# Scan exponentials with a per-head bias, forward rows alone shifted ahead of the choice, in a two-layer Hyena, SSD and attention backbone on one core

## The chip, the core and the metric

The kernel runs on one core of a Trainium2 chip, as one program in one launch. The metric is device time in microseconds (us). Five engines run side by side, each through a queue of its own in the order in which the built program lists its instructions: TensorE (PE), VectorE (DVE), ScalarE (ACT), GpSimd (POOL), and SyncE (SP), which issues nearly all DMAs here. They wait for each other through semaphores.

## What is computed

Two layers over 512 latent tokens and 256 context tokens, width 1024. Each layer projects its normalised input into three groups of heads (a Hyena long convolution, a bidirectional Mamba-2 scan, a windowed attention), gates and concatenates them, projects back and normalises. The change lies in the scan. For one direction the reference computes, in chunks of 128 tokens:

```python
da = (dt * a).reshape(b, nc, SSM_CHUNK, h)
acs = jnp.cumsum(da, axis=2)
seg = acs[:, :, :, None, :] - acs[:, :, None, :, :]
decay_ls = jnp.exp(jnp.where(lower, seg, -jnp.inf))
y_diag = jnp.einsum("bclhn,bcshn,bclsh,bcshp->bclhp", Cc, Bc, decay_ls, xd)
...
y_f, s_f = _ssd_scan(xs, dt[:, :, 0], a[0], Bh, Ch, init_f)
y_b, s_b = _ssd_scan(flip(xs), flip(dt[:, :, 1]), a[1], flip(Bh), flip(Ch), init_b)
return y_f + flip(y_b), s_f, s_b
```

Within a chunk the forward direction fills the triangle of pairs on one side of the diagonal and the reversed direction the other one. So one 128x128 matrix per head can hold both: forward exponents in the one triangle, reversed exponents in the other. The step size dt is put into the exponent as its logarithm.

## The kernel before

Activations lie with channels on partitions and tokens along the free axis. Every fp32 product runs as three products of rounded parts (a high part, made by ACT, line 178; a low part, made by DVE, line 179), so TensorE does most of its work in the input projection (`proj`, lines 461 and 463: PSUM tiles `pl` for 512 latent tokens, `pc` for 256 context tokens), each block with its own weights (`wr`, loaded by line 439, split into `wh` and `wl`).

`ssm_in` projects the scan's inputs, applies a short convolution (`conv`, lines 530 to 543: ACT copies `pl` and `pc` out of PSUM in lines 532 and 536 and scales in 538, DVE does lines 539 and 540) and works out small per-token tables in the tile `sc`, eight tables of 128 x 96: 96 columns are 2 directions x 6 chunks x 8 heads, direction 0 (forward) in columns 0 to 47. Table 3 (`S2`, read as `LB`) is log(dt) minus the running sum of dt*a. The running sums as rows go to DRAM (`rd`).

`ssm` first scans the chunk states (lines 798 to 807), then takes the chunks one by one: 6 in layer 0, 4 in layer 1. A chunk makes `gm` (line 819, ACT) and `ys` (lines 829 to 838, DVE), transposes `ys` into the PSUM tile `py` (line 840), and then goes twice, for 4 heads each, through what is called a **pass** here:

1. SP loads `R` (128 partitions x 2 directions x 4 heads x 128, 512 KB) from `rd` (line 844). `R` has three buffers, so the load of a pass waits until the pass three before it has been read by line 854.
2. ACT adds `LB` to each head's rows, one instruction per direction and head (line 849, 8 in a pass).
3. DVE overwrites the reversed rows by the forward rows in the upper triangle (line 851).
4. ACT takes the exponential of all 4 heads at once (line 852, in place).
5. DVE multiplies with `gm` into `M` (line 854); then the buffer of `R` is free.
6. PE multiplies with x into `py` (line 858, 4 matmuls).

After both passes ACT copies `py` out (line 859) and SP stores it (line 860). There are 12 passes in layer 0 and 8 in layer 1. A scheduler sets the order of each engine's queue when the program is built: it places the instructions of all open work, so the scan's chunks stand between projections of the Hyena blocks (`hy_in`) and pieces of the next modulation (`modulation`, line 370; its 1 MB weight loads are line 365). A queue doesn't pass over an instruction that waits. Passes are told apart by the number of their buffer; in layer 0 before, passes 1 to 12 are R_833, 835, 846, 848, 861, 863, 876, 878, 891, 893, 906 and 908.

Of the kernel before, what the change touches and what calls it, by code (L numbers as in the profile page):

```python
# [12 lines left out]
AF = mybir.ActivationFunctionType  # L13
ALU = mybir.AluOpType
# [32 lines left out]
class Net:  # L47
# [642 lines left out]
    def ssm_in(self, l, xt, last):  # L690
        nc = self.nc
# [43 lines left out]
        X, Z, S, S2, DT, AC, TOT, DA = [sc[:, i] for i in range(8)]  # L735
# [39 lines left out]
        nc.vector.tensor_scalar_max(S2, DT, 1e-38)  # L775
        nc.scalar.activation(S2, S2, AF.Ln)
        nc.vector.tensor_tensor(S2, S2, AC, op=ALU.subtract)
        return xT, bt, bc, sc, rd

    def ssm(self, l, xT, bt, bc, sc, rd, last):  # L780

        nc = self.nc
        sp = self.dr.tile([4, P, QW], F32, name=self.nm("sp"))
        col = lambda c: c * P + (0 if c < 4 else 1)
        vec = lambda i, d, c: sc[:, i, (d * 6 + c) * 8:(d * 6 + c) * 8 + 8]
        W, EX, ET, LB, DT = 0, 1, 2, 3, 4
        h64 = lambda t: t.rearrange("p (h d) -> p h d", h=8)
        bc64 = lambda v: v.unsqueeze(2).to_broadcast([P, 8, 64])
        states = {}

        def scan(d, order):
            cur = None
            for i, c in enumerate(order):
                states[d, c] = cur
                if i == len(order) - 1:
                    break
                xw = self.w("xw", [P, 512], bufs=2)
                nc.vector.tensor_tensor(h64(xw), h64(xT[:, c]), bc64(vec(W, d, c)), op=ALU.mult)
                ps = self.wk()
                for g in range(2):  # L800
                    nc.tensor.matmul(ps[:, 256 * g:256 * g + 256], lhsT=bt[:, g, c], rhs=xw[:, 256 * g:256 * g + 256], start=True, stop=True)  # L801
                nxt = self.w(f"st{d}", [P, 512], bufs=5 if d else 3)
                if cur is None:
                    nc.vector.tensor_copy(nxt, ps)
                else:
                    nc.vector.tensor_tensor(h64(nxt), h64(cur), bc64(vec(ET, d, c)), op=ALU.mult)
                    nc.vector.tensor_tensor(nxt, nxt, ps, op=ALU.add)
                cur = nxt

        scan(1, [5, 4, 3, 2, 1, 0])  # L810
        scan(0, [4, 5, 0, 1, 2, 3])
        dcol = self.row[:, l, 40:48]
        for c in (0, 1, 2, 3) if last else (4, 5, 0, 1, 2, 3):
            q0 = col(c)
            pg = self.wk()
            for g in range(2):
                nc.tensor.matmul(pg[:, g * P:(g + 1) * P], lhsT=bc[:, g, q0:q0 + P], rhs=bc[:, 2 + g, q0:q0 + P], start=True, stop=True)
            gm = self.w("gm", [P, 2, P], bufs=2)
            nc.scalar.activation(gm, pg[:, 0:256].rearrange("p (g l) -> p g l", g=2), AF.Copy)

            own = self.ts([P, 10])
            for g in range(2):
                t = self.w("dg", [P, P])
                nc.vector.scalar_tensor_tensor(t, gm[:, g], 1.0, self.ident, op0=ALU.mult, op1=ALU.mult, accum_out=own[:, 8 + g:9 + g])
                w = slice(4 * g, 4 * g + 4)
                nc.vector.scalar_tensor_tensor(own[:, w], vec(DT, 1, c)[:, w], own[:, 8 + g:9 + g], dcol[:, w], op0=ALU.mult, op1=ALU.add)
            py = self.wk()
            ys = self.w("ys", [P, 512], bufs=3)
            nc.vector.tensor_tensor(h64(ys), h64(xT[:, c]), bc64(own[:, 0:8]), op=ALU.mult)
            for d in range(2):  # L830
                if states[d, c] is None:
                    continue
                po = self.wk()
                for g in range(2):
                    nc.tensor.matmul(po[:, 256 * g:256 * g + 256], lhsT=bc[:, 2 + g, q0:q0 + P], rhs=states[d, c][:, 256 * g:256 * g + 256], start=True, stop=True)
                yo = self.w("yo", [P, 512], bufs=3)
                nc.vector.tensor_tensor(h64(yo), h64(po), bc64(vec(EX, d, c)), op=ALU.mult)
                nc.vector.tensor_tensor(ys, ys, yo, op=ALU.add)
            for j in range(4):
                nc.tensor.matmul(py[:, j * P:(j + 1) * P], lhsT=ys[:, j * P:(j + 1) * P], rhs=self.ident, start=j == 0, stop=False, is_transpose=True, skip_group_check=True)  # L840

            for g in range(2):
                R = self.w("R", [P, 2, 4, P], bufs=3)
                nc.sync.dma_start(R, rd[:, 8 * c + 4 * g:8 * c + 4 * g + 4].partition_broadcast(P))
                for d in (1, 0):
                    for h in range(4):
                        hh = 4 * g + h
                        bias = vec(LB, d, c)[:, hh:hh + 1]
                        nc.scalar.activation(R[:, d, h], R[:, d, h], AF.Identity, bias=bias)  # L849
                E = R[:, 1]  # L850
                nc.vector.copy_predicated(E, self.upper.unsqueeze(1).to_broadcast([P, 4, P]), R[:, 0])
                nc.scalar.activation(E, E, AF.Exp)
                M = self.w("M", [P, 4, P], bufs=2)
                nc.vector.tensor_tensor(M, E, gm[:, g].unsqueeze(1).to_broadcast([P, 4, P]), op=ALU.mult)
                for h in range(4):
                    hh = 4 * g + h
                    r0, j = 64 * (hh % 2), hh // 2
                    nc.tensor.matmul(py[r0:r0 + 64, j * P:(j + 1) * P], lhsT=xT[:, c, 64 * hh:64 * hh + 64], rhs=M[:, h], start=False, stop=True, skip_group_check=True)
            nc.scalar.activation(bc[:, :, q0:q0 + P], py.rearrange("p (j l) -> p j l", j=4), AF.Copy, scale=0.5)
            nc.sync.dma_start(sp[:, :, q0:q0 + P].rearrange("j p t -> p j t"), bc[:, :, q0:q0 + P])  # L860
        return sp
# [504 lines left out]
```

## Time and profile before

| What | Value |
|---|---|
| runs | 1272.0, 1271.32 and 1279.13 us, median 1272.0 |
| profiled execution, its own time | 1275.1 us |
| profiled execution, span of the trace | 1273.2 us |
| mean granted TensorE clock | 0.986 |
| PE busy | 1206.8 us (95%) |
| DVE busy | 938.8 us (74%) |
| ACT busy | 613.2 us (48%) |
| POOL busy | 130.0 us (10%) |
| line 849, the adds | 160 instructions, 50.1 us, mean 391 ns |

Busy time is the time in which an engine had an instruction in work; matmuls overlap each other, so a busy PE can still be slow. The clock is the share of TensorE's full speed that was granted: 1.00 is 2.4 GHz, and the lower level is 1.2 GHz.

### The profile page before, as it was taken

To read this page: it belongs to the slowest core of one execution; us is meant where nothing else is said; L and a number is where in the kernel's file an instruction comes from. 1 tells how busy PE (TensorE), PEld (TensorE's weight loads), DVE (VectorE), ACT (ScalarE), POOL (GpSimd) and SP (SyncE) were. 2 spreads that over 40 slices of the span, in tenths; PEclk is the share of its full clock that TensorE was granted. 3 is DMA by queue.
4 is the path that set the end of the run, shared out by engine and by line. 5 is a ranking of instruction groups with operands and counts; after the bars stand their busy time and mean duration, and the time that the engine had idled before them with its cause. 6 is when DMAs were issued, how large, how long until landed. Compare 5 with 4: busy or idle time off the path is not lost.

```text
span 1273.2 us, 19331 instructions
## 1 busy us (share of the span) xinstructions
PE 1206.8 (95%) x6966; PEld 971.0 (76%) x6966; DVE 938.8 (74%) x1916; ACT 613.2 (48%) x1223; POOL 130.0 (10%) x117
## 2 busy tenths in 40 slices
PE   5988999999999999999989998999999998999997
PEld 3656788778777867799877777887887686898786
DVE  6986844978655875399856899768777498598577
ACT  5557623767436374333324454446754527433340
POOL 1421110000000000022110232100000000011102
PEclk9988999999999999999999999999999899999999
DMA  6776363312117468844689743442123726955872
GB/s 234 247 264 202 108 207 100 84 51 67 42 51 234 143 202 290 289 140 137 171 262 285 257 158 116 108 116 59 34 75 110 223 70 182 300 151 189 273 250 83
DMA packets 109193, 208.95 MB, mean 164 GB/s; under 512 B 10553, under 2 KB 55033, under 8 KB 109096
## 3 DMA queue, kind: packets, MB, share of 16 engines
q1 hardware_dynamic: 109096, 207.70, 52.2%
q8 instruction: 55, 0.90, 0.3%
q14 instruction: 42, 0.34, 0.1%
HBM read 162.44 MB, written 38.41 MB: 158 GB/s over the span
## 4 chain that ended last, share of the span: by engine, by line
PE 62%; DVE 11%; DMA 10%; issue 9%; ACT 5%; POOL 2%; SPq 1%; POOLq 0%; DVEq 0%; ACTq 0%
PE pl L461 23%; PE pc L463 8%; PE wk L183 4%; PE wk L184 4%; PE wk L185 4%; PE wk L682 3%; PE wk L671 3%; DMA R<-rd 3%; PE wk L633 2%; DMA wo<-in_w_out_dram 2%; PE wk L643 1%; PE wk L370 1%; ACT wh L178 1%; DMA wr<-in_w_in_dram 1%; PE wk L801 1%
## 5 line engine op out<-in xcount | busy, mean ns | idle before, releaser
L461 PE MATMUL pl<-Q,wh 128*128 128x512 f32 x1168 | 412.1, 404 | 0.8 <-ACT wh L178 0.4
L461 PEld LDWEIGHTS pl<-Q,wh 128*128 128x128 f32 x1168 | 219.2, 190 | 57.0 <-issue 12.7
L461 PE MATMUL pl<-Q,wl 128*128 128x512 f32 x584 | 233.4, 400 | 0.0
L463 PE MATMUL pc<-Q,wh 128*128 128x256 f32 x704 | 183.3, 290 | 4.1 <-DVE V L474 3.8
L178 ACT ACTIVATE wh<-wr 128x1024 fp32r<-128x1024 f32 x76 | 80.4, 1058 | 153.4 <-PE pc L463 74.3
L179 DVE TENSOR_TENSOR wl<-wr,wh 128x1024 fp32r<-128x1024 f32 x76 | 101.2, 1334 | 50.1 <-ACT wh L178 49.9
L463 PEld LDWEIGHTS pc<-Q,wh 128*128 128x128 f32 x704 | 126.2, 189 | 12.0 <-DVE V L474 5.5
L461 PEld LDWEIGHTS pl<-Q,wl 128*128 128x128 f32 x584 | 111.1, 190 | 24.3 <-issue 2.2
L946 POOL TENSOR_TENSOR ta<-ta 128x256 f32<-128x256 f32 x40 | 31.7, 792 | 706.2 <-DVE ta L944 421.2
L463 PE MATMUL pc<-Q,wl 128*128 128x256 f32 x352 | 101.0, 287 | 0.0
L463 PEld LDWEIGHTS pc<-Q,wl 128*128 128x128 f32 x352 | 66.7, 189 | 1.8 <-issue 1.2
L849 ACT ACTIVATE R<-R,sc 128x128 f32<-128x128 f32 x160 | 50.1, 391 | 22.9 <-DMA R<-rd 22.9
L648 ACT ACTIVATE pr<-wk,S 128x512 f32<-128x512 f32 (+2 forms) x80 | 48.2, 608 | 14.0 <-DVE S L647 13.5
L646 DVE TENSOR_REDUCE S<-wk 128x1 f32<-128x512 f32 (+2 forms) x80 | 45.1, 578 | 9.3 <-PE wk L644 7.4
L178 ACT ACTIVATE wh<-wo 128x1024 fp32r<-128x1024 f32 x30 | 31.6, 1057 | 39.1 <-DMA wo<-in_w_out_dram 18.7
L179 DVE TENSOR_TENSOR wl<-wo,wh 128x1024 fp32r<-128x1024 f32 x30 | 38.6, 1290 | 10.8 <-ACT wh L178 10.6
L671 PE MATMUL wk<-con,pr 128*128 128x128 f32 x320 | 45.1, 276 | 0.0
L671 PEld LDWEIGHTS wk<-con,pr 128*128 128x128 f32 x320 | 36.2, 140 | 8.1 <-issue 4.2
L178 ACT ACTIVATE yh<-ta 128x512 fp32r<-128x512 f32 x32 | 20.1, 629 | 43.4 <-DVE ta L947 43.4
L183 PE MATMUL wk<-ph,Q 128*128 128x256 f32 x144 | 39.8, 288 | 0.8 <-ACT ph L178 0.8
L184 PE MATMUL wk<-plo,Q 128*128 128x256 f32 x144 | 39.7, 283 | 0.5 <-DVE plo L179 0.5
L185 PE MATMUL wk<-ph,Q 128*128 128x256 f32 x144 | 39.5, 281 | 0.0
(403 smaller groups left out, 2875.1 us busy)
## 6 DMA issues: line engine op xcount, KB each, us to landing
wr<-in_w_in_dram SPq DMA_DIRECT2D x76, 512.0 KB, 4.0
Q<-in_w_mod_dram SPq DMA_DIRECT2D x24, 1024.0 KB, 6.8
wo<-in_w_out_dram SPq DMA_DIRECT2D x43, 512.0 KB, 5.2
kd<-k SPq DMA_DIRECT2D x40, 256.0 KB, 2.3
R<-rd SPq DMA_DIRECT2D x20, 512.0 KB, 7.6
kt<-kd SPq DMA_DIRECT2D x40, 256.0 KB, 2.9
sp<-V SPq DMA_DIRECT2D x20, 384.5 KB, 3.7
cs<-sp SPq DMA_DIRECT2D x60, 128.0 KB, 4.6
```

The source lines that it names most:

```text
L178: nc.scalar.activation(hi, src, AF.Copy)
L179: (nc.gpsimd if lo_on == "p" else nc.vector).tensor_tensor(lo, src, hi.bitcast(F32), op=ALU.subtract)
L183: mm(out, lhsT=lh, rhs=rh, start=start, stop=False, **k)
L184: mm(out, lhsT=lh, rhs=rl, start=False, stop=False, **k)
L185: mm(out, lhsT=ll, rhs=rh, start=False, stop=stop, **k)
L461: nc.tensor.matmul(pl, lhsT=w[:, k * P:(k + 1) * P], rhs=x[:, 0:SEQ], start=s, stop=e)
L463: nc.tensor.matmul(pc[:, 0:CTX], lhsT=w[:, k * P:(k + 1) * P], rhs=x[:, SEQ:SEQ + CTX], start=s, stop=e)
L646: nc.vector.tensor_reduce(m[:, h:h + 1], sa[:, :ws], axis=AX.X, op=ALU.max)
L648: nc.scalar.activation(pr[:, h, :ws], sa[:, :ws], AF.Exp, bias=negm[:, h:h + 1], scale=0.125, accum_out=sums[:, h:h + 1])
L671: turned = nc.tensor.transpose(ps[:, (2 * g + h) * P:(2 * g + h + 1) * P], prs[g][:, hp + h, i * P:(i + 1) * P], self.ident)
L682: m = nc.tensor.matmul(pv[r0:r0 + 64, hp * P:hp * P + 256], lhsT=vt[:, keys[i], r0:r0 + 64], rhs=pts[i][:, g], start=i == 0 and hp == 0, s ...
L849: nc.scalar.activation(R[:, d, h], R[:, d, h], AF.Identity, bias=bias)
```

## The change

The table `LB` gets one more step: its forward half becomes the difference of the forward and the reversed half. In a pass, only the forward rows get an addition (4 instructions rather than 8). The choice then takes shifted forward rows or raw reversed rows, and the exponential adds the reversed half of `LB` as its bias, which differs by head, so it is 4 instructions of 128 columns rather than 1 of 512. exp(raw + LB1) for reversed rows and exp(raw + LB0 - LB1 + LB1) for forward rows are what stood there before.

```diff
@@ ssm_in
         nc.scalar.activation(S2, S2, AF.Ln)
         nc.vector.tensor_tensor(S2, S2, AC, op=ALU.subtract)
+
+        nc.vector.tensor_tensor(S2[:, 0:48], S2[:, 0:48], S2[:, 48:96], op=ALU.subtract)
         return xT, bt, bc, sc, rd
@@ ssm
-                for d in (1, 0):
-                    for h in range(4):
-                        hh = 4 * g + h
-                        bias = vec(LB, d, c)[:, hh:hh + 1]
-                        nc.scalar.activation(R[:, d, h], R[:, d, h], AF.Identity, bias=bias)
+                for h in range(4):
+                    nc.scalar.activation(R[:, 0, h], R[:, 0, h], AF.Identity, bias=vec(LB, 0, c)[:, 4 * g + h:4 * g + h + 1])
                 E = R[:, 1]
                 nc.vector.copy_predicated(E, self.upper.unsqueeze(1).to_broadcast([P, 4, P]), R[:, 0])
-                nc.scalar.activation(E, E, AF.Exp)
+                for h in range(4):
+                    nc.scalar.activation(E[:, h], E[:, h], AF.Exp, bias=vec(LB, 1, c)[:, 4 * g + h:4 * g + h + 1])
                 M = self.w("M", [P, 4, P], bufs=2)
```

The scheduler places everything anew from there on, so the order changes on all queues but POOL's behind the first pass. In the changed kernel the adds are line 848, the choice is line 850 and `gm` is line 821; line numbers from 852 on are as before. Three places follow.

ACT in layer 0, passes 6 and 7 (before R_863 and R_876, now R_863 and R_876 too), between them the convolution of a Hyena block (lines 532, 536 and 538) and a weight split (line 178). Before:

```order
L849 ACTIVATE R_863_4394<-R_863_4394,sc_751_3781 128x128 x8
L849 ACTIVATE R_876_4445<-R_876_4445,sc_751_3781 128x128 x8
L532 ACTIVATE U_925_4751<-pl_922_4700 128x512
L852 ACTIVATE R_863_4394<-R_863_4394 128x512
L852 ACTIVATE R_876_4445<-R_876_4445 128x512
L819 ACTIVATE gm_866_4417<-wk_865_4414 128x256
L536 ACTIVATE U_925_4751<-pc_923_4701 128x256
L178 ACTIVATE wh_948_4923<-wr_947_4921 128x1024
L859 ACTIVATE Q_679_3138<-wk_855_4357 128x4x128
L538 ACTIVATE V_924_4750<-U_925_4751,par_75 128x769
```

The same place on ACT of the changed kernel:

```order
L848 ACTIVATE R_863_4390<-R_863_4390,sc_751_3781 128x128 x4
L848 ACTIVATE R_876_4440<-R_876_4440,sc_751_3781 128x128 x4
L532 ACTIVATE U_925_4740<-pl_922_4689 128x512
L536 ACTIVATE U_925_4740<-pc_923_4690 128x256
L178 ACTIVATE wh_948_4912<-wr_947_4910 128x1024
L538 ACTIVATE V_924_4739<-U_925_4740,par_75 128x769
L852 ACTIVATE R_863_4390<-R_863_4390,sc_751_3781 128x128 x4
L821 ACTIVATE gm_866_4412<-wk_865_4409 128x256
L852 ACTIVATE R_876_4440<-R_876_4440,sc_751_3781 128x128 x4
L848 ACTIVATE R_878_4457<-R_878_4457,sc_751_3781 128x128 x2
L859 ACTIVATE Q_679_3138<-wk_855_4354 128x4x128
L848 ACTIVATE R_878_4457<-R_878_4457,sc_751_3781 128x128 x2
```

The exponentials of pass 6 moved behind line 536, the weight split and line 538, and those of pass 7 behind line 821 as well.

DVE at the same place, where line 854 is the product that frees pass 6's buffer. Before:

```order
L854 TENSOR_TENSOR M_862_4388<-R_861_4376,gm_851_4348 128x512
L838 TENSOR_TENSOR ys_856_4358<-ys_856_4358,yo_860_4369 128x512
L851 COPY_PREDICATED R_863_4394<-upper_83,R_863_4394 128x512
L851 COPY_PREDICATED R_876_4445<-upper_83,R_876_4445 128x512
L854 TENSOR_TENSOR M_864_4406<-R_863_4394,gm_851_4348 128x512
L824 SCALAR_TENSOR_TENSOR dg_868_4420,S_867_4419<-gm_866_4417,con_73 128x128
```

The same place on DVE of the changed kernel:

```order
L854 TENSOR_TENSOR M_862_4384<-R_861_4373,gm_851_4345 128x512
L840 TENSOR_TENSOR ys_856_4355<-ys_856_4355,yo_860_4366 128x512
L850 COPY_PREDICATED R_863_4390<-upper_83,R_863_4390 128x512
L850 COPY_PREDICATED R_876_4440<-upper_83,R_876_4440 128x512
L539 SCALAR_TENSOR_TENSOR V_924_4739<-U_925_4740,par_75,V_924_4739 128x769
L179 TENSOR_TENSOR wl_949_4913<-wr_947_4910,wh_948_4912 128x1024
L854 TENSOR_TENSOR M_864_4401<-R_863_4390,gm_851_4345 128x512
L826 SCALAR_TENSOR_TENSOR dg_868_4415,S_867_4414<-gm_866_4412,con_73 128x128
```

A convolution step (line 539) and a weight split (line 179) now stand ahead of pass 6's product.

ACT in layer 0, passes 8 to 11 (R_878, R_891, R_893 and R_906). Before:

```order
L849 ACTIVATE R_878_4463<-R_878_4463,sc_751_3781 128x128 x8
L849 ACTIVATE R_891_4514<-R_891_4514,sc_751_3781 128x128 x4
L852 ACTIVATE R_878_4463<-R_878_4463 128x512
L819 ACTIVATE gm_881_4486<-wk_880_4483 128x256
L849 ACTIVATE R_891_4514<-R_891_4514,sc_751_3781 128x128 x4
L849 ACTIVATE R_893_4532<-R_893_4532,sc_751_3781 128x128 x2
L859 ACTIVATE Q_679_3138<-wk_870_4426 128x4x128
L849 ACTIVATE R_893_4532<-R_893_4532,sc_751_3781 128x128 x6
L178 ACTIVATE wh_958_4997<-wr_957_4995 128x1024
L852 ACTIVATE R_891_4514<-R_891_4514 128x512
L849 ACTIVATE R_906_4583<-R_906_4583,sc_751_3781 128x128
L852 ACTIVATE R_893_4532<-R_893_4532 128x512
```

The same place on ACT of the changed kernel:

```order
L848 ACTIVATE R_891_4507<-R_891_4507,sc_751_3781 128x128 x3
L852 ACTIVATE R_878_4457<-R_878_4457,sc_751_3781 128x128 x4
L821 ACTIVATE gm_881_4479<-wk_880_4476 128x256
L848 ACTIVATE R_891_4507<-R_891_4507,sc_751_3781 128x128
L848 ACTIVATE R_893_4524<-R_893_4524,sc_751_3781 128x128 x3
L859 ACTIVATE Q_679_3138<-wk_870_4421 128x4x128
L848 ACTIVATE R_893_4524<-R_893_4524,sc_751_3781 128x128
L178 ACTIVATE wh_958_4986<-wr_957_4984 128x1024
L532 ACTIVATE U_933_4812<-pl_930_4761 128x512
L848 ACTIVATE R_906_4574<-R_906_4574,sc_751_3781 128x128 x2
L852 ACTIVATE R_891_4507<-R_891_4507,sc_751_3781 128x128 x4
L852 ACTIVATE R_893_4524<-R_893_4524,sc_751_3781 128x128 x4
```

Pass 8's exponentials stand behind adds of pass 9 as before; pass 9's moved behind the first adds of pass 11, where before only pass 10's stood.

## Rows read from the trace of the kernel before

**Rows 1.** The page's first part: busy time, share of the span, instructions of each engine.
```profile
PE 1206.8 (95%) x6966; PEld 971.0 (76%) x6966; DVE 938.8 (74%) x1916; ACT 613.2 (48%) x1223; POOL 130.0 (10%) x117
```

**Rows 2.** Timeline of PE: start, duration, [idle before <-releaser]; scan products of passes.
```profile
450.51 0.66 PE L858 MATMUL wk<-M,Q 128*64 128x128 f32 x8 [2.90 <-DVE M L854]
...
461.80 0.66 PE L858 MATMUL wk<-M,Q 128*64 128x128 f32 x8
...
469.72 0.66 PE L858 MATMUL wk<-M,Q 128*64 128x128 f32 x8
...
477.04 0.66 PE L858 MATMUL wk<-M,Q 128*64 128x128 f32 x8
478.65 0.66 PE L858 MATMUL wk<-M,Q 128*64 128x128 f32 x8 [0.95 <-DVE M L854]
...
1071.97 0.66 PE L858 MATMUL wk<-M,Q 128*64 128x128 f32 x8 [2.85 <-DVE M L854]
```

**Rows 3.** Busy time by stretch; after the engines stand PEclk, DMA share, GB/s.
```profile
451.00:454.00 3.00, 3.00 (x14) 2.52 (x11) 3.00 (x9) 2.53 (x7) 0.00 (x0) 0.68 0.66 139
454.00:456.00 2.00, 2.00 (x12) 0.81 (x11) 2.00 (x4) 1.42 (x6) 0.00 (x0) 0.62 0.69 195
...
1072.00:1076.00 4.00, 4.00 (x18) 3.20 (x19) 3.85 (x12) 4.00 (x11) 0.00 (x0) 0.66 0.20 66
```

**Rows 4.** Timeline of ACT in layer 0, passes 4 to 11.
```profile
447.64 1.57 ACT L849 ACTIVATE R<-R,sc 128x128 f32<-128x128 f32 x5 [2.88 <-DMA R<-rd]
...
455.62 2.45 ACT L849 ACTIVATE R<-R,sc 128x128 f32<-128x128 f32 x8 [0.58 <-DMA R<-rd]
...
458.46 1.14 ACT L852 ACTIVATE R<-R 128x512 f32<-128x512 f32 x2
...
463.93 3.62 ACT L849 ACTIVATE R<-R,sc 128x128 f32<-128x128 f32 x12
...
476.95 0.40 ACT L849 ACTIVATE R<-R,sc 128x128 f32<-128x128 f32 x1 [2.11 <-DMA R<-rd]
```

**Rows 5.** Timeline of DVE: choice and product of pass 4, products of passes 6 and 10.
```profile
445.08 0.73 DVE L851 COPY_PREDICATED R<-upper,R 128x512 f32<-128x512 uint8 x1
449.76 0.69 DVE L854 TENSOR_TENSOR M<-R,gm 128x512 f32<-128x512 f32 x1 [3.95 <-ACT R L852]
...
459.10 0.69 DVE L854 TENSOR_TENSOR M<-R,gm 128x512 f32<-128x512 f32 x1 [0.23 <-ACT R L852]
...
477.90 0.69 DVE L854 TENSOR_TENSOR M<-R,gm 128x512 f32<-128x512 f32 x1 [2.05 <-ACT R L852]
```

**Rows 6.** Groups of lines, 395 to 500 us: count | busy us, mean ns | idle before.
```profile
L849 ACT ACTIVATE R<-R,sc 128x128 f32<-128x128 f32 x96 | 29.9, 391 | 11.1 <-DMA R<-rd 11.1
...
L179 DVE TENSOR_TENSOR wl<-wr,wh 128x1024 fp32r<-128x1024 f32 x7 | 8.5, 1220 | 9.0 <-ACT wh L178 8.9
...
L852 ACT ACTIVATE R<-R 128x512 f32<-128x512 f32 x12 | 7.3, 624 | 2.0 <-DVE R L851 1.9
L538 ACT ACTIVATE V<-U,par 128x769 f32<-128x769 f32 x7 | 7.2, 1031 | 0.2
L539 DVE SCALAR_TENSOR_TENSOR V<-U,par,V 128x769 f32<-128x769 f32 x7 | 7.1, 1018 | 2.3 <-ACT V L538 2.3
...
L178 ACT ACTIVATE wh<-wr 128x1024 fp32r<-128x1024 f32 x6 | 6.3, 1056 | 18.5 <-PE pc L463 18.5
```

**Rows 7.** Views of lines 777 and 844: durations min/median/max; DMA from issue to landing.
```profile
L777 DVE TENSOR_TENSOR sc<-sc x2: 242/242/242, 389.1 to 980.2; 128x96 f32<-128x96 f32 x2
...
DMA to landing us min/median/max: 4.9/7.6/8.5
```

**Rows 8.** Timeline of SP's queue: R's loads of passes 8, 9, 11; layer 1, pass 7.
```profile
456.91 3.28 SPq L844 DMA_DIRECT2D R<-rd  x2
...
469.16 0.36 SPq L844 DMA_DIRECT2D R<-rd  x1
...
1060.36 0.36 SPq L844 DMA_DIRECT2D R<-rd  x1
```

## Prediction

> **What bounds the kernel now.** The page's first part comes first: PE is busy for 1206.8 of 1273.2 us, ACT for 613.2 [rows 1]. The kernel is a chain of matmuls, and ACT's work costs time only where PE waits for it. So the timeline of PE through both scans was read next. PE waits for the scan's products three times by more than half a microsecond: 2.90 us for pass 4 and 0.95 us for pass 10 of layer 0, 2.85 us for pass 6 of layer 1 [rows 2], together 6.70 us. The busy times by stretch add the price behind a wait: after both long waits PE runs at a granted clock of 0.62 to 0.68, so near its lower level of 1.2 GHz, for some 5 us [rows 3]. That loses about 3 x 0.32 + 2 x 0.38 = 1.7 us in the two rows of layer 0, and 1.4 us in the one of layer 1; I take 2 us for a wait of nearly 3 us. After the wait of 0.95 us no such stretch follows. The scan's waits thus cost 6.7 + 4 = 10.7 us, and more than that the change can't win in the scan.
>
> Then what each wait is for. In all three PE waits for the product of line 854, that for the exponential, and the exponential stood in ACT's queue behind adds of a later pass whose load had not landed. Pass 4 shows it best: its choice ended at 445.08 + 0.73 = 445.81, ACT then sat 2.88 us for pass 5's load, did five adds, and only then came the exponential, so that the product began at 449.76 [rows 4, 5]. For pass 10 it was one add of pass 11, at 476.95 [rows 4]. Altogether ACT waits 11.1 us for loads of R in layer 0 [rows 6]. The loop to watch is therefore: product of pass n, load of pass n + 3 into its buffer, 4.9 to 8.5 us until it has landed [rows 7], adds, and behind those the exponential of a pass in between.
>
> **The change, part by part.**
>
> *ACT's work.* Twelve adds in a row take 3.62 us [rows 4], so one follows the other by (3.62 - 0.39)/11 = 0.294 us. Two 512-wide exponentials take 1.14 us, so the second adds 1.14 - 0.62 = 0.52. A pass is 8 x 0.294 + 0.52 = 2.87 us before. No row shows a 128-wide exponential with a bias; it lies between the add of the same width and bias (0.294) and the 512-wide one (0.52). I take 0.294, because shape and bias are those of the add. A pass then takes 8 x 0.294 = 2.35 us, 0.52 less, over 20 passes 10.4 us less ACT work (at the upper end 0.4 more in a pass, 8 us more ACT work). None of it is time by itself: ACT is idle for half of the span, and in the scan it waits for loads. The Trainium skill, page "ScalarE: Activation LUTs", section "What ACT_TABLE_LOAD costs", gives 280 ns + 0.833 ns per column for an activation with a pointer bias and an overlap of 93 ns, whatever the function. By it the estimate is 387 - 93 = 294 ns for the exponential as well, and the sum would be the same 10.4 us; the trace has no such exponential.
>
> *From landing to product.* Before: 8 adds 2.45, choice 0.73, exponential 0.62, together 3.80 us. After: 1.27 + 0.73 + 1.27 = 3.27 us. So a buffer could come free 0.53 us sooner, if nothing else stood between.
>
> *The extra step on the table* is one DVE instruction per layer, half as wide as the one of line 777 with 0.242 us [rows 7]. The first pass's adds come 8 us later, behind a load. Cost 0; without that cover 0.24 us each.
>
> *What stands between now.* Nothing new is waited for, but queues have another order. Three places in layer 0, then layer 1, worked by hand from rows:
>
> - Pass 4: exponential behind five adds of pass 5 before, behind three now. 447.64 + 3 x 0.294 + 1.27 = 449.8, against 449.76 before. The wait stays, less 0.35 us of projection that PE now has ahead of it: 2.55 us.
> - Pass 6: the adds of pass 7 start at 455.62 and now take 1.18. Then lines 532, 536, 178 and 538 come ahead of the exponential: 0.48 + 0.28 + 0.95 + 0.94 (each mean less the overlap of 0.1 [rows 6]) to 459.5. The exponentials end at about 460.7, where both passes' ended at 459.6 before [rows 4]. On DVE lines 539 (1.02) and 179 (1.13 behind it) stand ahead of the product: 459.5 + 1.0 + 1.1 = 461.6, against 459.10 [rows 5, 6]. PE reaches this product at 461.80 before [rows 2] and hardly waits now. But the product ends at 462.3, and that is when pass 9's load can start, 2.5 us later than before: the second load of the SP row began at 456.91 + 3.28 - 0.36 = 459.8 [rows 8].
> - Passes 8 to 12: pass 9's load took at most 6.5 us before, since the twelve adds ran through, the ninth at 463.93 + 8 x 0.294 = 466.3 [rows 4]. Its landing now is the unknown: 4.9 at the least, 7.6 at the median [rows 7]. I take the middle, 6.25, because both kinds occur around here. Landed 468.55; three adds to 469.4; exponential of pass 8 to 470.7; product to 471.4. PE arrives at about 469.8 (469.72 before): wait 1.65. That product's end starts pass 11's load (469.16 before [rows 8]); landed 477.65, two adds, then pass 9's exponential to 479.5, product to 480.2. PE needs about 6.4 us from pass 8 to pass 9 in the new order (7.3 before [rows 2], less 0.9 of matmuls put behind): it arrives at 477.9 and waits 2.35. Pass 12's load follows at 480.2 and leaves some 0.5 us of wait at pass 11.
>
> Waits in layer 0: 2.55 + 1.65 + 2.35 + 0.5 = 7.05, against 3.85: +3.2. A wait of 2.35 lies between one without a slow stretch (0.95) and one with (2.85); I count half of the 2 us: +1. With landings of 4.9 the same steps give waits of 2.55, 0.35, 1.8 and 0: +0.9 and no slow stretch. With 7.6 they give 2.55, 3.05, 3.8 and 1.9: +7.5, and two slow stretches more, +11.5.
>
> - Layer 1: pass 4's product now has line 539 ahead of it, so pass 7's load (1060.36 before [rows 8]) starts about 0.6 us later; the adds of pass 7, which stand ahead of pass 6's exponential as before, save 1.2; a weight split moved ahead of the exponential (1.0) and another with line 540 ahead of the product. PE has about 0.7 us more work ahead of it. The wait of 2.85 stays within half a microsecond. Taken as 0; bounds -4.9 (the wait and its slow stretch gone) and +2.
>
> *Behind the scans* the queues keep another order as well, to the end of each layer. No view of before prices that. Its size I bound by the single waits that I have, 1 to 3 us in either direction per layer, so 4 us to either side, and take 0.
>
> **Sum.** 0 (ACT) + 0 (table) + 4.2 (layer 0) + 0 (layer 1) + 0 (behind) = +4.2 us on the profiled execution's 1275.1 us, which is its span of 1273.2 and 1.9 around it: 1279.3. That execution lies 3.1 us above the median of the runs, 1272.0, so the forecast for the median is 1276. A measurement of this kernel can tell about 1%, 12.7 us, from no change.
>
> **The rivals.**
>
> 1. *Nothing that can be measured, at 1272 or a little below.* Landings near 4.9 us, as idle queues would give: +0.9 in layer 0, layer 1 up to 2 us better. 1270 to 1273. For it: ACT has less to do and each chain is 0.53 shorter. Against: the median landing is 7.6.
> 2. *Faster, the waits vanish.* If shorter chains let each load start early enough, all 10.7 us go: 1261. For it: every wait hangs on this loop. Against: the order, where exponentials still stand behind adds of later passes; and even then it is under 1%. It passes 1% only with 2 us more from behind the scans.
> 3. *Slower by over 1%.* One mechanism: R's landings in passes 8 to 12. Between 4.9 and 7.6 us of landing, the loop's price grows from 0.9 to 11.5 us, 3.9 for each microsecond. At 7.6 it is 1283.5; from about 7.9 us on it passes 1284.7; at 8.5, the slowest load of the trace, 1287. For it: the median. Against: pass 9's load landed within 6.5 before, and pass 7's in about 5 (issued after pass 4's product, 450.45, landed at 455.6 [rows 4, 5]).
> 4. *It doesn't save ACT work,* since the narrow exponential costs the upper 0.52: four take 2.2 rather than 1.27 us, which lengthens the chain of each of five passes by 0.9: about +4 on top, 1280.
>
> The Trainium skill speaks for rivals 3 and 4 and against the change: page "TensorE: Matmul & The Clock Gate", the table of specifications at its head, calls ScalarE's queue strictly first in, first out. By that, four exponentials never pass an add that waits, as pass 4 shows in this trace (3.95 us between the choice and the product's start [rows 5]); an ACT queue that could pass would give rival 2's 1261.
>
> **How the numbers follow.** The forecast, 1273 to 1281: 0.45. Rival 1: 0.25. Rival 2: 0.08, of which half is faster by over 1%. Rival 3: 0.12, all but 0.02 slower by over 1%. Rival 4: 0.10, of which 0.02 is slower by over 1%. So faster 0.04, slower 0.12, within 1% 0.84. The range takes rivals 1 and 4 whole and the near parts of 2 and 3: 1265 to 1285.
>
> **What would show it.** Right: line 848 with 80 adds and line 852 with 80 exponentials of some 0.39 us, ACT's busy time down by about 12.6 us (20 times the 0.63 of line 852) without the span following; PE's wait at pass 4 still near 2.6 us; pass 6's product starting some 2 us later behind line 179; new PE waits of 1 to 3 us at passes 8 and 9 of layer 0; layer 1's wait near 2.8. Wrong: narrow exponentials near 0.6 us (the price); no wait at passes 8 and 9 (the landing, or my order of events); layer 1's wait gone; or a span that moves while the scans' waits don't, which would put the difference behind the scans.

## The result and the profile after

The changed kernel takes 1282.8 us (median of 15 runs, 1277.0 to 1285.1), the kernel before 1273.3 beside it (15 runs). The ratio is 1.0063, 95% interval [1.0047, 1.0079]: 8 us slower, inside 1%. The profiled execution has a span of 1281.7 us and a time of 1283.5 of its own.

The page's first part, to be held against [rows 1]:

```profile
PE 1212.3 (95%) x6966; PEld 978.4 (76%) x6966; DVE 939.6 (73%) x1918; ACT 602.6 (47%) x1203; POOL 130.4 (10%) x117
```

ACT has 10.6 us less to do, and the span is 8.5 us longer. PE shows 5.5 us more busy time with the same 6966 instructions, so part of the loss in this execution is matmuls that ran at a lower clock. Its mean granted clock, 0.979, is at the low end of the 15 executions (0.979 to 0.986, median 0.985); the kernel before was profiled at 0.986, and its 95 executions beside the experiments have medians of 0.985 to 0.987. So the profiled pair shows more of the clock than a usual pair: by the medians it is at most some 0.002 of 1280 us, 2.6 us by estimate, of the 8. The groups of lines in 395 to 500 us (count | busy us, mean ns | idle before) have half the additions of [rows 6] and four times the exponentials:

```profile
L848 ACT ACTIVATE R<-R,sc 128x128 f32<-128x128 f32 x48 | 15.8, 391 | 18.2 <-DMA R<-rd 18.2
...
L852 ACT ACTIVATE R<-R,sc 128x128 f32<-128x128 f32 x48 | 15.2, 389 | 3.0 <-DVE R L850 3.0
```

A narrow exponential with a bias costs 389 ns, an addition of the same shape 391. ACT now waits 18.2 us for R's loads where it waited 11.1. The view of line 846, R's loads, from issue to landing, which was 4.9/7.6/8.5 [rows 7]; in both traces it rests on four of the 20 loads, those of passes 3, 6, 10 and 13:

```profile
DMA to landing us min/median/max: 7.1/7.8/8.4
```

The timeline of PE (start, duration, [idle before <-releaser]), to be held against [rows 2]: passes 4 and 9 of layer 0's scan, the waits of a projection (line 463) in the scan and behind it, one of the Hyena part (line 183), and one in each of layer 1's scan and the stretch behind it.

```profile
449.07 0.66 PE L858 MATMUL wk<-M,Q 128*64 128x128 f32 x8 [2.71 <-DVE M L854]
...
456.18 0.50 PE L463 MATMUL pc<-Q,wh 128*128 128x256 f32 x2 [1.33 <-ACT U L536]
...
478.01 1.12 PE L858 MATMUL wk<-M,Q 128*64 128x128 f32 x8 [2.10 <-DVE M L854]
...
523.60 0.51 PE L463 MATMUL pc<-Q,wh 128*128 128x256 f32 x2 [1.08 <-DVE V L474]
...
544.95 0.39 PE L183 MATMUL wk<-Q,yh 128*128 128x256 f32 x1 [3.03 <-ACT yh L178]
...
1077.63 0.55 PE L858 MATMUL wk<-M,Q 128*64 128x128 f32 x6 [1.86 <-DVE M L854]
...
1106.69 0.69 PE L926 MATMUL wk<-con,fo 128*128 128x128 f32 x2 [3.39 <-DMA fo<-sp]
```

Passes 6, 8, 10, 11 and 12 of layer 0 show no wait. Now busy time by stretch (length, then busy time of PE, PEld, DVE, ACT, POOL; PEclk, DMA share, GB/s), first of the kernel before, then of the changed one:

```profile
440.00:495.00 55.00, 51.14 (x327) 38.53 (x326) 41.54 (x93) 38.64 (x102) 0.00 (x0) 0.97 0.73 209
495.00:575.00 80.00, 76.82 (x522) 67.03 (x521) 48.20 (x95) 25.32 (x41) 8.22 (x10) 1.00 0.72 238
```

```profile
450.00:460.00 10.00, 8.67 (x55) 6.25 (x54) 8.46 (x16) 8.50 (x24) 0.00 (x0) 1.00 0.82 232
...
475.00:480.00 5.00, 2.90 (x15) 2.01 (x14) 2.74 (x6) 4.61 (x15) 0.00 (x0) 0.80 0.82 238
480.00:485.00 5.00, 5.00 (x31) 4.14 (x30) 4.00 (x10) 1.94 (x5) 0.00 (x0) 0.86 0.90 232
525.00:530.00 5.00, 5.00 (x23) 4.36 (x22) 0.32 (x5) 1.40 (x2) 0.00 (x0) 0.66 0.95 324
545.00:550.00 5.00, 5.00 (x27) 4.76 (x28) 5.00 (x9) 2.13 (x3) 1.02 (x2) 0.66 0.81 258
440.00:495.00 55.00, 48.85 (x318) 37.28 (x317) 39.78 (x88) 34.17 (x93) 0.00 (x0) 0.97 0.74 195
495.00:575.00 80.00, 74.68 (x483) 64.84 (x483) 43.80 (x84) 22.26 (x35) 7.48 (x10) 0.96 0.74 233
```

Busy time times clock is what PE did, in microseconds at full speed. From 440 to 575 us that is 49.6 + 76.8 = 126.4 before and 47.4 + 71.7 = 119.1 after: 7.3 us less done. Of this 4.4 are waits (11.5 us idle where 7.0 were) and 3.0 the clock behind the scan, which fell to 0.66 twice there and never in the kernel before. By milestones of the two traces (start of the scan's table at line 757, last product of line 858, the wait of line 964 near 570 us), layer 0's scan is 1.6 us longer and the stretch behind it, to line 964, 5.2 us. The rest nearly cancels: -1.5 up to the scan, where both run the same instructions, +1.6 up to layer 1's scan, -0.8 in it, +2.3 behind it. In this pair of executions most of the loss is made from 440 to 575 us. PE's waits for the scan's products did not grow in all: 2.71, 2.10 and 1.86 are 6.7 us, as 2.90, 0.95 and 2.85 were before.

### The profile page after: what moved, and what is told of

Same layout as the page of the kernel before. It is cut to its first block, busy times and chain, and to the rows that moved or that the text cites. A ratio compares the mean times of both kernels' runs of the same rounds, so it can differ in the third digit from the quotient of the medians.

```text
span 1281.7 us, 19321 instructions
## 1 busy us (share of the span) xinstructions
PE 1212.3 (95%) x6966; PEld 978.4 (76%) x6966; DVE 939.6 (73%) x1918; ACT 602.6 (47%) x1203; POOL 130.4 (10%) x117
## 5 line engine op out<-in xcount | busy, mean ns | idle before, releaser
L848 ACT ACTIVATE R<-R,sc 128x128 f32<-128x128 f32 x80 | 26.5, 391 | 31.9 <-DMA R<-rd 31.8
```

The costliest lines, as they stand in the source:

```text
L848: nc.scalar.activation(R[:, 0, h], R[:, 0, h], AF.Identity, bias=vec(LB, 0, c)[:, 4 * g + h:4 * g + h + 1])
```

## Experiments

The change does two things: it alters ACT's work, and it lets the scheduler choose another order for nearly all that follows. To part them, a table in the kernel pins the order of issue of every engine, SP's queue included, by dependencies that order issue and add no wait:

```diff
+ORDER = (
...
+def pin(tc):
+    import base64, json, zlib
+    per = {}
+    for i in tc.nc.cur_bb.bb.instructions:
+        if "PoolBoundary" not in type(i).__name__:
+            per.setdefault(str(i.engine).split(".")[-1], []).append(i)
+    info = mybir.DependencyInfo(mybir.DependencyClass.NoSync, mybir.DependencyReason.DATA)
+    for e, chains in json.loads(zlib.decompress(base64.b64decode(ORDER))).items():
+        for runs in chains:
+            q = [per[e][x] for s, n in runs for x in range(s, s + n)]
+            for x, y in zip(q, q[1:]):
+                tc.add_manual_dep(y, x.name, info, reason="order")
...
     net.phase(None)
+    pin(tc)
```

No run pins a kernel to its own order and changes nothing else. But the traces of the changed kernel, which is not pinned, and of E9, which is, hold the same number of semaphore instructions, 1525, so the pins added no waiting instruction there.

"Old order" is that of the kernel before, "new order" that of the changed one; "old work" and "new work" are their instructions. Three chips were used, for E1 to E4, E5 to E8 and E9 to E12; each ratio is to the kernel before on the same chip.

| run | work | order | R | median us | ratio [95%] |
|---|---|---|---|---|---|
| the change | new | new | 3 | 1282.8 | 1.0063 [1.0047, 1.0079] |
| E1 | new | old | 3 | 1271.6 | 0.9979 [0.9961, 0.9997] |
| E2 | old | new | 3 | 1288.5 | 1.0108 [1.0078, 1.0138] |
| E3 | new | old to the end of scan 0, then new | 3 | 1274.8 | 1.0006 [0.9987, 1.0025] |
| E4 | new | old to layer 1's scan, then new | 3 | 1271.4 | 0.9975 [0.9955, 0.9994] |
| E5 | new | old to pass 6, then new | 3 | 1281.2 | 1.0051 [1.0030, 1.0073] |
| E6 | new | new to pass 6, then old | 3 | 1273.7 | 1.0003 [0.9985, 1.0021] |
| E7 | new | new | 4 | 1275.9 | 1.0007 [0.9987, 1.0026] |
| E8 | new | old | 4 | 1269.5 | 0.9967 [0.9949, 0.9985] |
| E9 | new | new, two inversions undone | 3 | 1275.5 | 1.0007 [0.9987, 1.0027] |
| E10 | new | old, two inversions put in | 3 | 1274.2 | 1.0006 [0.9985, 1.0027] |
| E11 | new | old, exponentials first | 4 | 1270.2 | 0.9962 [0.9940, 0.9983] |
| E12 | old | old, exponentials first | 4 | 1272.7 | 0.9986 [0.9970, 1.0001] |

### E1 and E2: work or order

E1 expected: 

> The changed kernel's instructions (four additions and four narrow exponentials a pass, the table step), pinned engine by engine, DMA queue included, into the order in which the kernel before issues its own: the four narrow exponentials stand where the wide one stood, the forward additions where they stood, the rest as before. The pins order issue only and add no wait of their own. Theory A (the slow-down is the new order that the scheduler chose around the change, most of it behind the scans): the time goes back to that of before or a little under, 1268 to 1274 us, since ACT has 10 us less work and its waits in the scan stand in the old places. Theory B (the operations themselves do it: the exponentials behind additions that wait for R's loads, the buffer of R held longer): it stays at 1279 to 1284. Theory C (the landings of R's loads differ from execution to execution and the order does not matter): something between, with an interval that holds both 1272 and 1282.

E2 expected: 

> The other corner: the instructions of the kernel before (eight additions, one wide exponential a pass, no table step), pinned into the order of the changed kernel: the eight additions stand where its four stand, the wide exponential where the first narrow one stands. Theory A (order): 1280 to 1286 us, as slow as the changed kernel, or slower by ACT's 10 us more where that shows in the scan. Theory B (operations): 1270 to 1275, as before. Theory C: between.

Measured: 0.9979 and 1.0108. The order makes the kernel slow and the new work makes it faster in either order: by 0.2% in the old one (E1, whose interval ends just below 1), by 1.0063/1.0108, so 0.45%, in the new one. With the new work, the new order costs 0.84% against the old one (1.0063/0.9979). Theory A holds; E2's 1288.5 lies above its 1280 to 1286; PE's wait for line 536 at pass 7 is 2.49 us there, 1.33 in the changed kernel, since eight additions stand ahead of line 536.

### E3 to E6: which stretch of the order

E3 expected: 

> The changed kernel's instructions, in the old order up to the last multiplication of layer 0's scan (line 858) and in the new order from there. Theory A with the split that the two traces show (the new order costs 1.9 us in layer 0's scan, about 5 behind it up to line 517, 1.3 at line 425, a gain of 1.7 in layer 1's scan, 4 to 5 behind that): only the first share goes, so 1278 to 1282 us. If instead the scan's own order sets off what follows (the stretch behind it is slow because it starts late or in another state): 1271 to 1275.

E4 expected: 

> The changed kernel's instructions, in the old order up to the last transcendental step ahead of layer 1's scan (line 757) and in the new order from there. Theory A by the shares of the traces: what is left is layer 1, -1.7 us in the scan and 4 to 5 behind it, so 1272 to 1277 us, and the wait of the first transposes behind the scan for their loads (3.4 us at 1106.7 in the changed kernel) is still there. If layer 1's loss only follows from layer 0's: 1268 to 1272.

E3 fell on the other side: 1274.8, not 1278 to 1282. With the old order up to the last product of layer 0's scan most of the loss is gone, though the new order rules everything behind it. Most of what the trace placed behind the scan is set off inside it; 0.27% is left against E1. E4's 1271.4 equals E1's 1271.6, so the new order of layer 1 costs nothing that shows. That takes away a cause that I had read from the trace: PE's wait for line 918's loads, which stand further back in SP's queue in the new order. E4 keeps it (timeline of PE):

```profile
1094.20 1.07 PE L926 MATMUL wk<-con,fo 128*128 128x128 f32 x5 [3.17 <-DMA fo<-sp]
```

E5 expected: 

> The changed kernel's instructions, in the old order up to the M of pass 6 (line 854, sixth time in layer 0's scan) and in the new order from there. The run with the old order to the end of layer 0's scan was as fast as the kernel before, so the loss is set off inside that scan. Theory A (its root is what stands ahead of pass 6's exponentials in the new order: lines 536, 178 and 538 of a projection, and pass 7's additions that wait for R's load, so that R's buffer comes free late, pass 9's load lands late, and line 463 waits for line 536): 1272 to 1276 us, no wait of PE at line 463 for line 536, pass 9's wait under 1 us. Theory B (the root is behind pass 6: pass 9's exponentials stand behind two additions of pass 11 that wait for their load): 1279 to 1283, pass 9's wait at 1.5 us or more.

E6 expected: 

> The complement: the changed kernel's instructions in the new order up to the M of pass 6, in the old order from there. Theory A (root ahead of pass 6's exponentials): 1277 to 1282 us, since line 463's wait of 1.3 us, pass 9's late load and what the clock takes behind them stay. Theory B (root behind pass 6): 1271 to 1275, with the waits of passes 9 to 12 at 1 us or less in all.

Theory B in both: the root is behind pass 6's product. The new order from there on is slow (E5, 1.0051, pass 9's wait 2.81 us), the new order up to there is not (E6, 1.0003). So lines 536, 178 and 538 ahead of pass 6's exponential, on which my prediction built its longest step, are not where most of the cost comes from. A smaller share may lie there: E6 is 0.24% above E1, hardly more than the intervals, and its trace does not have PE's wait at line 463, 1.33 us in the changed kernel, so E6 does not price that wait.

### E7 and E8: R's ring of buffers

```diff
-                R = self.w("R", [P, 2, 4, P], bufs=3)
+                R = self.w("R", [P, 2, 4, P], bufs=4)
```

E7 expected: 

> The changed kernel in its own order, pinned, with four buffers for R in place of three, so that a load of R waits for the M of four passes ago and not of three. Theory A (the waits in the scan are the ring of R's buffers: load, additions, choice, exponentials, M, next load): PE's waits for M at passes 4 and 9 (2.7 and 2.1 us) go, in layer 1's scan the 1.9 us too, line 463's wait (behind pass 7's additions, which wait for their load) shrinks; with the slow-clock stretches that follow such waits 1270 to 1275 us. Theory B (the loads are late because of what stands ahead of them on SP's queue or because the transfers themselves are slow, not because of the buffer): the waits stay over 1 us each, 1279 to 1283 us.

E8 expected: 

> The changed kernel's instructions in the old order, with four buffers for R. This version is meant to beat both. Theory A (ring of R's buffers): pass 4's wait of 2.5 us with the slow stretch behind it (1.7 us) and layer 1's 1.9 us go: 1265 to 1269 us. Theory B (queue or transfer): 1270 to 1273 us, as with three buffers in this order.

With a fourth buffer the new order falls from 1.0063 to 1.0007, just above its range. The view of line 858, for PE alone, gives its waits for M over the whole kernel (us, times), with three buffers and with four:

```profile
  DVE M L854: 6.7, 3
...
  DVE M L854: 2.7, 2
```

Pass 9's wait is gone, but pass 4's stayed, at 2.46 us, in E7 and at 2.76 in E8, against theory A: the exponential stands there behind an addition of pass 5 whose load is still on its way. In the old order the fourth buffer brings 0.1%, less than the intervals; E8's 1269.5 lies between its two theories.

### E9 and E10: two inversions on ACT

What differs on ACT behind pass 6? The timeline of ACT in the changed kernel, to be held against [rows 4], and under it that of SP's queue, R's loads of passes 9 and 11, against [rows 8]:

```profile
462.50 0.68 ACT L848 ACTIVATE R<-R,sc 128x128 f32<-128x128 f32 x2
465.85 0.99 ACT L848 ACTIVATE R<-R,sc 128x128 f32<-128x128 f32 x3 [2.67 <-DMA R<-rd]
466.74 1.26 ACT L852 ACTIVATE R<-R,sc 128x128 f32<-128x128 f32 x4
...
471.64 1.00 ACT L848 ACTIVATE R<-R,sc 128x128 f32<-128x128 f32 x3 [3.04 <-DMA R<-rd]
...
475.36 0.69 ACT L848 ACTIVATE R<-R,sc 128x128 f32<-128x128 f32 x2 [0.51 <-DMA R<-rd]
475.96 2.44 ACT L852 ACTIVATE R<-R,sc 128x128 f32<-128x128 f32 x8
```

```profile
460.81 0.36 SPq L846 DMA_DIRECT2D R<-rd  x1
...
468.76 0.36 SPq L846 DMA_DIRECT2D R<-rd  x1
```

Pass 8's exponentials (466.74) stand behind three additions of pass 9, which wait for a load issued at 460.81; those of passes 9 and 10 (475.96) behind two additions of pass 11, whose load could only be issued when pass 8's late product had freed the buffer (468.76). With the new work in the old order (E1) neither is so: all four additions of pass 9 and of pass 11 come behind those exponentials. In the kernel before itself, four of pass 9's eight additions did stand ahead of pass 8's exponential, without a wait, since their load had landed (the twelve additions at 463.93 in [rows 4]). E9 undoes both on ACT alone, the three other engines and SP's queue keep the new order (p is the pass):

```diff
 848 p8 x2
-848 p9 x3
 852 p8 x4
+848 p9 x3
...
-848 p11 x2
 852 p9 x4
 852 p10 x4
+848 p11 x2
```

E9 expected: 

> The changed kernel in its own order, pinned, with two edits on ACT alone in the second half of layer 0's scan: pass 8's four exponentials are issued ahead of the three additions of pass 9, which wait 2.67 us for R's load, and those of passes 9 and 10 ahead of the two additions of pass 11, which wait 0.51 us. All other engines keep the new order. Theory A (these two inversions are the cause: an exponential whose data are there stands behind an addition whose load has not landed, and M, and with it the next load, come late): 1273 to 1278 us, PE's wait at pass 9 from 2.1 to 1 us or less. Theory B (the cause is the order of the other engines there: PE, DVE or SP's queue): 1280 to 1283 us.

E10 expected: 

> The converse: the changed kernel's instructions in the old order, with the same two inversions put in on ACT alone: three additions of pass 9 ahead of pass 8's exponentials, two additions of pass 11 ahead of those of passes 9 and 10. Theory A (the inversions are the cause): PE waits for M at passes 8 to 10, 2 us or more in all, and the time goes from 1271.6 to 1276 to 1282 us. Theory B: 1270 to 1273 us as without them.

E9: 1.0007. Moving five additions takes back 0.56%, some 7 us, two thirds of what the new order costs; theory A, with a wait of 1.07 us at pass 9 for its 1 us or less. Which of the two inversions weighs more was not tried. Its timelines of ACT and PE, and its busy time by stretch:

```profile
465.27 1.28 ACT L852 ACTIVATE R<-R,sc 128x128 f32<-128x128 f32 x4 [2.27 <-DVE R L850]
466.45 0.97 ACT L848 ACTIVATE R<-R,sc 128x128 f32<-128x128 f32 x3
...
474.44 2.44 ACT L852 ACTIVATE R<-R,sc 128x128 f32<-128x128 f32 x8
476.78 0.68 ACT L848 ACTIVATE R<-R,sc 128x128 f32<-128x128 f32 x2
```

```profile
476.49 0.66 PE L858 MATMUL wk<-M,Q 128*64 128x128 f32 x8 [1.07 <-DVE M L854]
```

```profile
525.00:530.00 5.00, 5.00 (x33) 4.47 (x32) 0.06 (x1) 1.67 (x3) 0.00 (x0) 1.00 0.98 336
440.00:495.00 55.00, 49.83 (x331) 38.02 (x330) 41.11 (x89) 34.07 (x93) 0.00 (x0) 1.00 0.73 212
495.00:575.00 80.00, 76.03 (x512) 65.62 (x512) 48.41 (x97) 25.31 (x41) 9.01 (x11) 1.00 0.73 230
```

The exponentials start 1.5 us sooner and the additions no longer wait at either place. PE's wait at pass 9 falls from 2.10 to 1.07 us, and PE does 49.8 + 76.0 = 125.9 us of work from 440 to 575, 6.8 more than in the changed kernel. Of that gain only 2.3 us are waits; in this pair of executions the larger part is the clock, which stays at 1.00 in both stretches. By the mean clocks of all executions it is not: their median is 0.985 in the changed kernel (15 executions, the profiled one 0.979) and 0.9865 in E9 (12, the profiled one 0.987). A difference of 0.0015 is 1.9 us of 1280, by estimate, so most of the 7 us must usually be something other than the clock, and no trace shows where.

E10: 1.0006, on theory A's side of E1's 0.9979 but under its range, at 1274.2. Put into the old order, the same two inversions cost 0.27% rather than 0.56%, about as much as the intervals can tell; PE waits 2.02 and 0.51 us for M. They do not make the old order as slow as the new one: their price depends on the rest of the order.

### E11 and E12: a better version

On ACT, the exponentials of passes 4, 16 and 18 come ahead of the additions behind which they stood in the old order too, with four buffers for R:

```diff
 848 p4 x4
-848 p5 x1
 852 p4 x4
+848 p5 x1
...
 848 p16 x4
+852 p16 x4
 848 p17 x4
...
-852 p16 x4
```

E11 expected: 

> A version meant to beat both: the changed kernel's instructions in the old order with four buffers for R, and on ACT the exponentials of passes 4, 16 and 18 ahead of the additions of the pass behind them, which wait for R's load (3.4 us ahead of pass 5's, 3.07 us ahead of pass 19's with four buffers). Theory A: PE's waits for M at pass 4 (2.76 us with four buffers) and pass 18 (0.6 to 1.9 us) go, with what the clock takes behind them: 1264 to 1268 us. Theory B (the waits move to the next pass, as its additions are as late as before): 1268 to 1271 us, as with four buffers alone.

E12 expected: 

> The kernel before with what the last version has besides the change: its own order, pinned, four buffers for R, and the wide exponentials of passes 4, 16 and 18 ahead of the additions of the pass behind them. Against the last version it gives the worth of the change itself in a good order. Theory A (ACT's 10 us less are worth little, as 0.2% in the old order, since ACT is not the bound): 2 to 4 us above the last version, 1267 to 1271 us. Theory B (with the inversions gone ACT's work no longer matters at all): the same as the last version within 1 us.

E11 is 0.9962 and beats the kernel before. Pass 4's wait is gone, yet the time is that of E8, 0.9967, within the intervals. In layer 1 waits came up instead: PE waits 1.90 us for M at pass 18, where E8 has 0.58, and 1.82 us at pass 16 for a convolution step (line 531), where E8 has none. So the waits moved, as theory B has it. Against E12, 0.9986, the change itself is worth 0.24%, 2.6 us, inside E12's 2 to 4 (E12's 1272.7 lies above its 1267 to 1271), but the intervals overlap, so this isn't shown. Nor are the two orders quite alike: E12 still has additions of the reversed rows of passes 9, 11 and 12 ahead of exponentials of the pass before.

## Why the prediction was right, and where not

The forecast was 1276, with 1265 to 1285; it came to 1282.8, within 1% as the likeliest case said, and above the forecast's own 1273 to 1281. That it stayed inside the range is in part luck: the room above 1281 was there for rival 3, slow landings, and another step moved the time.

- **ACT's work, -10.4 us, hidden.** The size is right: 10.6 less, narrow exponentials at 389 ns beside additions at 391, so rival 4 falls. The Trainium skill, page "ScalarE: Activation LUTs", section "What ACT_TABLE_LOAD costs", gave 387 by estimate, and the trace agrees with 389. "Hidden" was nearly right: E1 shows a gain of 0.21%, E11 against E12 0.24%, so some 3 us, at the edge of the intervals. The 12.6 us that the prediction named as a sign was too much, since it left out the overlap of instructions in a row that the 10.4 counts.
- **The extra step on the table, 0.** No run takes it apart; nothing in the profile waits for it.
- **Layer 0's scan, +4.2.** The order of events came as worked out. All events lie 1.5 us earlier, since that execution's start does. Pass 6's product began at 460.10 behind line 179 (461.6 forecast), and pass 9's load was issued at 460.81. ACT began pass 9's additions 5.0 us later, so the load landed near the lower bound of 4.9 and not at the middle taken, 6.25; the DMA engines were busy for 0.84 of that time, so it did not take the idle queues of rival 1. Pass 11's load took 6.6 us (468.76 to 475.36). The 4.9 and 7.6 that the working took as least and median come from four loads of 20. For the lower bound the working gave waits of 2.55, 0.35, 1.8 and 0 at passes 4, 8, 9 and 11; the trace has 2.71, 0, 2.10 and 0. It missed one: line 463 waits 1.33 us for line 536, which stands behind pass 7's additions. To the scan's end the loss is 1.6 us, with PE's waits up by 2.3, for the 4.2 forecast. Rival 3's mechanism, slow landings, did not decide.
- **Layer 1's scan, 0.** Within its bounds: -0.8 us in the profile, and E4 equals E1. The wait did not stay within half a microsecond: 1.86 for 2.85.
- **Behind the scans, 0 within 4.** This is the step that failed: a mis-sized term. Behind layer 0's scan alone the profile has +5.2 us, 2.1 of them waits and some 3 the clock (less of it the clock in the other executions, as the medians above say); with +1.6 up to layer 1's scan and +2.3 behind that it comes to 9.1, where 0 within 4 to a side was taken. And it is not a term by itself, as the sum had it. E3 keeps the new order there and loses little, E9 moves five additions within the scan and most of it goes. The prediction named the inversions, exponentials of passes 8 and 9 behind additions that wait, and priced them by the waits that they cause at once; in the profiled pair most of their price came 30 to 70 us later.
- **Of what would show it wrong,** the last held: the span moved by 8.5 us, while PE's waits for the scans' products stayed at 6.7 us in all and only line 463's 1.33 us came on top.

The step behind the failed one was a rule that I had drawn from two waits: a slow stretch follows a wait of nearly 3 us, and none follows one of 1 us. It does not hold, as the last section shows.

Open is how five additions at 466 to 476 us lead to a lower clock at 526 and 545. The changed kernel, E2, E5 and E7, the four with both inversions and the new order behind them, show a clock of 0.66 to 0.73 somewhere from 525 to 550 us, and the kernel before and the other nine runs none; but that is one execution of each. Of the others only the mean clock is known: its median is 0.982 to 0.985 in those four and 0.9845 in E3, and 0.9865 to 0.9875 in the other eight runs, so those four do run at a lower clock than most others, worth 2 to 7 us by estimate (0.0015 to 0.0055 of 1280). The rest of the loss, and the 0.28% between E9 and E1, were not traced to their places.

## What to carry to other kernels

Where a scheduler decides the order, a small change has two effects, its work and the order that it sets off, and they can have opposite signs: issue the new work in the old order, and the old work in the new, before judging either. On an in-order engine, work whose data are there goes ahead of work that waits for a load, above all when it frees the buffer that the next load needs. And price such an inversion by more than its own wait: here moving five additions took 1 us off PE's wait at pass 9 and 7 us off the time.

## What was not expected of the hardware

A wait's length alone does not tell whether PE's clock falls behind it. In the changed kernel the 2.71 us at 449.07 and the 1.33 at 456.18 left it at 1.00 up to 460, while in the kernel before 2.90 us at the same pass brought it to 0.68 [rows 2, 3], and behind the 1.08 at 523.60 it fell to 0.66. The same wait at line 183 was 2.80 us in E3 and 2.98 in E7 (timeline of PE, then busy time by stretch, E3 first):

```profile
536.62 0.38 PE L183 MATMUL wk<-Q,yh 128*128 128x256 f32 x1 [2.80 <-ACT yh L178]
```

```profile
540.00:545.00 5.00, 5.00 (x41) 4.76 (x40) 4.92 (x10) 1.75 (x3) 0.74 (x1) 1.00 0.62 179
```

```profile
538.24 0.39 PE L183 MATMUL wk<-Q,yh 128*128 128x256 f32 x1 [2.98 <-ACT yh L178]
```

```profile
540.00:545.00 5.00, 5.00 (x30) 4.79 (x28) 3.48 (x6) 2.74 (x5) 1.47 (x2) 0.70 0.61 175
```

Nothing was lost behind the one, and 0.30 x 5 = 1.5 us behind the other, so a forecast to within 0.5% has to leave room for a few such stretches. And with a fourth buffer (E7) the four loads of R that the view has took 7.1/8.2/10.4 us from issue to landing, where they took 7.1/7.8/8.4 with three: pass 6's load was issued 2.3 us sooner (439.80 for 442.12) and landed 0.2 us sooner (450.24 for 450.48).
